# An FFN whose gate and up products run on blocks without the 1/rms factor: one direct chunk instead of two, weight sums by accumulating DMA

## The chip, the cores and the metric

The kernel runs on one core of a Trainium2 chip. The metric is the device time of one execution in microseconds (us); smaller is better. The engines are named as the profile names them: PE (TensorE, matrix products), PEld (its weight loads), DVE (VectorE), ACT (ScalarE), POOL (GpSimd, here used almost only to issue DMAs, among them those that add to what lies in SBUF), and SP (SyncE, which issues plain DMAs).

## The reference

One layer of a streaming encoder over 512 positions of 1024 channels: three token mixers, gated and merged, an output projection with residual, then a SwiGLU FFN with residual. The change is in the FFN and at its seam with the output projection:

```python
D_MODEL = 1024; SEQ = 512; D_FF = 2816
...
x = x + jnp.einsum('bsd,de->bse', merged, w_out[l])

h2 = rms_norm(x, norm_ffn[l])
act = jax.nn.silu(jnp.einsum('bsd,df->bsf', h2, w_ffn_gate[l])) * jnp.einsum('bsd,df->bsf', h2, w_ffn_up[l])
x = x + jnp.einsum('bsf,fd->bsd', act, w_ffn_down[l])
```

with `rms_norm(x, g) = x * rsqrt(mean(x*x) + EPS) * g`, all in float32. The factor 1/rms depends on the position alone, so it may stand before a product or behind it.

## The kernel before

Everything is held transposed: channels on the 128 partitions, the 512 positions along the free dimension. To reach float32 accuracy each operand is split into a high part (ScalarE copies it to `fp32r`) and a low part (VectorE subtracts the high part from the operand), and each product of two tiles is three matmuls: high by high, high by low, low by high. So every weight tile costs a ScalarE and a VectorE step over 128x1024 elements (`split_w` at line 111 and 112, `split_a` at 1403 and 1404), and PE runs three matmuls for each pair of 128x128 weights and 128 channels.

The weights go through a pool of three buffers (`wp`: `raw`, `whi`, `wlo`): a split can begin when the product three earlier has ended. `STEPS` and `OFF` shift the split weights inside their buffers: in each stage of 256-column matmuls the first four weight tiles lie 0, 4, 8 and 12 elements in, all later ones 16.

The output projection (loop over `c` in 0..3, 256 channels each) adds the residual (`x1`, line 1291), and forms x1 times `norm_ffn` without 1/rms as `h2` (high part on ScalarE, line 1294, low part on VectorE, 1295), along with the sum of squares. `rms2` turns this sum into `rb2`, the 1/rms of each position on all partitions, in the background of the first direct chunk.

The FFN's gate and up are made in 11 chunks of 256 hidden channels (of gate and of up each). Two kinds of chunk exist:

- **Direct**, the first `NDIRECT` = 2. `chan_chunk` runs gate (`ps_fg`) and up (`ps_fu`) on `h2`, 512 positions to a matmul: 96 matmuls of 512 columns. The outputs are scaled by `rb2`: gate once before the SiLU, up at the end.
- **Seven products** (`seven`), the other 9. The 256 hidden channels, the 1024 channels and the 512 positions are each halved, and the eight block products are replaced by seven (Winograd's variant of Strassen's scheme), named in `ORDER`: 11, 12, S2, S1, S3, S4, 22. The weight side of each is a block or a sum of blocks of w (S1..S4), for gate and up together; the other side is a block or difference of blocks of the normalised x1 (11, 21, 22, T1..T4: the map is `WITH`). A product is 24 matmuls of 256 columns into the PSUM tiles `ps_y` or `ps_x`; ScalarE copies banks out between products (`tx`, `ty`), and `finish_act` adds the last bank, applies SiLU to the gate and multiplies.

The blocks of the normalised x1 are prepared while PE runs the two direct chunks: background steps (`bg`, popped by `tick`) multiply by `rb2` (`norm2`, line 1336, 16 steps of 128x256), form T1..T4 (`diff_b`, 1347) and split all seven (`split_b`, 1341 and 1342). The weight blocks are loaded by SP, four blocks a chunk in two DMAs each (`load_a`, line 1378, into the eight buffers of `corner`), and their sums S1..S4 are four VectorE steps a chunk (`sums_a`, line 1385). `make_a` splits three products ahead in program order. The engines otherwise follow the order in which a scheduler puts the program's instructions, each engine in order, with weight splits and copies out of PSUM given priority.

Behind the FFN's chunks stands the down projection (`ps_d`, `ps_dx`, `ps_dy`), which already takes its weight sums from accumulating DMAs on POOL (`dadd`, line 1515).

Of the kernel before, what the change touches and what calls it, by code (L numbers as in the profile page):

```python
# [8 lines left out]
F32 = mybir.dt.float32  # L9
F32R = mybir.dt.float32r  # L10
# [16 lines left out]
EARLY = 300  # L27
WARM = 9
GBUFS = 27
NDIRECT = 2  # L30
KD = 10
NTICK = (1, 1)
H = S // 2
# [32 lines left out]

@with_exitstack
def layer_kernel(ctx: ExitStack, tc: tile.TileContext, x, xt, vecs, w_in, w_qkv7, w_gate7, w_pool, w_rg, w_ig,
                 w_branch, w_br7, w_out, w_fg, w_fu, w_fd, w_fd7, out):
    nc = tc.nc  # L70
    act = nc.scalar.activation
    dve = nc.vector
# [39 lines left out]
            dve.tensor_tensor(lo, raw, hi.bitcast(F32), ALU.subtract)  # L112
        return hi, lo

    def add_direct(key, src, a, b):
        def make(n):
            raw = wp.tile([P, a, b], F32, tag="raw", name="raw" + n)
            nc.sync.dma_start(raw, src)
            return split_w(raw, [P, a, b], n)
        specs.append((key, make))  # L120

    def add_chunk256(key, ap, c0):
        add_direct(key + (0,), cols(ap, 0, 4, c0, 256), 4, 256)
        add_direct(key + (1,), cols(ap, 4, 4, c0, 256), 4, 256)

    def add_gate(br, c):
        add_chunk256(("gate", br, c), w_in, 5120 + br * 1024 + c * 256)
# [1128 lines left out]
    with ExitStack() as ffn:  # L1256
# [14 lines left out]

        x1p = {}
        x1 = []
        h2 = []
        for c in range(4):
            xr = g4([2, S], f"xr{c}")
            nc.sync.dma_start(xr, xt[2 * c * P:(2 * c + 2) * P, :].rearrange("(j p) t -> p j t", p=P))
            if c == 0:
                psh = [chunk_psum(("out", n), fp) for n in range(2)]
                for half in range(2):  # L1280
                    for n in range(2):
                        half_chunk(psh[n], ("out", n), half, mt, 0, n == half == 0)
            pss = psh[c] if c < 2 else chan_chunk(("out", c), mt, pool=fp)
            hh = g4([2, S], f"h2h{c}", F32R)
            hl = g4([2, S], f"h2l{c}", F32R)
            for j in range(2):
                k = 2 * c + j
                if c % 2 == 0:
                    x1p[c // 2, j] = mp.tile([P, 2, S], F32, tag="m", name=f"x1{c}{j}")
                t = x1p[c // 2, j][:, c % 2, :]  # L1290
                dve.tensor_tensor(t, pss[j], xr[:, j, :], ALU.add)
                x1.append(t)
                gcol = vcol("norm_ffn", k)
                act(hh[:, j, :], t, AF.Copy, scale=gcol)
                dve.scalar_tensor_tensor(hl[:, j, :], t, gcol, hh[:, j, :].bitcast(F32), ALU.mult,
                                         ALU.subtract)
                h2.append((hh[:, j, :], hl[:, j, :]))
                if k == 0:
                    act(sqsum, t, AF.Square)
                else:  # L1300
                    sq = small(f"sq2{k}", 2, "sq2")
                    act(sq, t, AF.Square)
# [21 lines left out]

        BN = {}
        B = {}

        def norm2(k):  # L1330
            for j in range(2):
                b = BN.setdefault((k // 4, j), None)
                if b is None:
                    b = BN[k // 4, j] = corner([4, H], f"hn{k // 4}{j}")
                js = slice(j * H, (j + 1) * H)
                dve.scalar_tensor_tensor(b[:, k % 4, :], x1[k][:, js], vcol("norm_ffn", k),
                                         rb2[:, js], ALU.mult, ALU.mult)

        def split_b(nm, key, which=0):
            h, l = g4([4, H], f"B{which}{nm}h", F32R), g4([4, H], f"B{which}{nm}l", F32R)  # L1340
            act(h, BN[key], AF.Copy)
            dve.tensor_tensor(l, BN[key], h.bitcast(F32), ALU.subtract)
            B[which, nm] = h, l

        def diff_b(nm, x, y):
            BN[nm] = corner([4, H], f"hn{nm}")
            dve.tensor_tensor(BN[nm], BN[x], BN[y], ALU.subtract)

        def prepare_b():
            nrm = [lambda k=k: norm2(k) for k in range(8)]  # L1350
            return nrm[:4] + [lambda: split_b("11", (0, 0))] + nrm[4:] + [
                lambda: split_b("21", (1, 0)),
                lambda: diff_b("T1", (0, 1), (0, 0)),
                lambda: diff_b("T2", (1, 1), "T1"),
                lambda: split_b("T2", "T2"),
                lambda: split_b("T1", "T1"),
                lambda: diff_b("T3", (1, 1), (0, 1)),
                lambda: split_b("T3", "T3"),
                lambda: split_b("22", (1, 1)),
                lambda: diff_b("T4", (1, 0), "T2"),  # L1360
                lambda: split_b("T4", "T4")]

        SUMS = {"S2": (("S3", "11", "21", ALU.subtract), ("S2", "22", "S3", ALU.subtract)),
                "S1": (("S1", "21", "22", ALU.add),),
                "S4": (("S4", "12", "S2", ALU.subtract),)}

        DOWN = NF // 2
        steps = [(c, nm) for c in range(NDIRECT, DOWN) for nm in ORDER]
        raw = {}
        A = {}  # L1370
        made = [0, NDIRECT]
        offs = []

        def load_a(c):
            for nm in ("11", "21", "22", "12"):
                raw[c, nm] = t = corner([2, 4, P], f"w{c}_{nm}")
                for w in range(2):
                    nc.sync.dma_start(t[:, w], cols((w_fg, w_fu)[w], KH[nm] * 4, 4, c * 256 + CH[nm] * P, P))

        def sums_a(c, nm):  # L1380
            for s_, x, y, op in SUMS.get(nm, ()):
                if (c, s_) in raw:
                    continue
                raw[c, s_] = t = wp.tile([P, 2, 4, P], F32, tag="raw", name=f"w{c}_{s_}")
                dve.tensor_tensor(t, raw[c, x], raw[c, y], op)
# [12 lines left out]

        def split_a(src, n):
            o = offs.pop(0) if offs else OFF  # L1400
# [36 lines left out]
        def seven(c):  # L1437
# [13 lines left out]
            for n, (nm, ps, half, first, t, ts_, src, ss) in enumerate(plan):  # L1451
                make_a(n0 + n + 3)
                product(A.pop((c, nm)), B[0, WITH[nm]], ps, half, first, True)
                if t is not None:
                    act(t[:, :, ts_], src[:, :, ss], AF.Copy)
                if c == DOWN - 1 and nm in PRE:
                    split_d2("11", PRE.index(nm), 0, 0)
                if nm == "S4":
                    finish_act(tx, X, a[:, 0, :])
                if nm == "22":  # L1460
                    finish_act(ty, Y, a[:, 1, :])
            acts.append(a)

        bg.extend([lambda: None, rms2] + prepare_b())
        for c in range(NDIRECT):
            pg = chan_chunk(("fg", c), h2, 3, fp)
            pu = chan_chunk(("fu", c), h2, 3, fp)
            if c == NDIRECT - 1:
                make_a(3)
            a = g4([2, S], f"act{c}")  # L1470
            for j in range(2):
                sg = small(f"sg{c}{j}", 2, "sq2")
                dve.tensor_tensor(sg, pg[j], rb2, ALU.mult)
# [171 lines left out]


_INS = ["x", "xt", "vecs", "w_in", "w_qkv7", "w_gate7", "w_pool", "w_rg", "w_ig", "w_branch", "w_br7", "w_out",
        "w_ffn_gate", "w_ffn_up", "w_ffn_down", "w_down7"]


# [41 lines left out]
```

## Time and profile before

| | before |
|---|---|
| three runs | 898.22, 898.73, 899.13 us; median 898.73 |
| profiled execution, first to last instruction (span) | 896.5 us |
| median less span | 2.2 us |
| PE busy | 891.2 us, 99% |
| PE weight load busy | 795.2 us, 89% |
| VectorE busy | 739.4 us, 82% |
| ScalarE busy | 528.5 us, 59% |
| POOL busy | 88.8 us, 10% |
| granted TensorE clock | 1.00 |

The profiled execution has no device time of its own beside its span: the three runs were made apart from it. The chain that ended last is followed back from the last instruction of the program; where it runs on PE without a gap, PE sets the time there. A PE row's duration in the timeline is the latency of a pipelined matmul: the spacing is the difference between two starts.

### The profile page before, as it was taken

What the parts mean: (1) busy time and instruction counts of PE and PEld (TensorE: products, weight loads), DVE (VectorE), ACT (ScalarE), POOL (GpSimd) and SP (SyncE); (2) the same over time, 40 slices, a digit from 0 to 9 for tenths busy, and PEclk for the clock granted to TensorE, in tenths of its full rate; (3) what the DMA queues carried; (4) which work ended last, traced back from release to release, by engine and by line L of the source; (5) the groups of instructions that cost most, each with busy time, mean ns of one, the idle gap of its engine ahead of it and who ended that gap; (6) DMA issues with size and microseconds to landing.
All of it is one profiled execution on the core that took longest, in us unless ns stands there. A gap on an engine that the chain in (4) does not pass through costs nothing.

```text
span 896.5 us, 14227 instructions
## 1 busy us (share of the span) xinstructions
PE 891.2 (99%) x5563; PEld 795.2 (89%) x5563; DVE 739.4 (82%) x934; ACT 528.5 (59%) x730; POOL 88.8 (10%) x130
## 2 busy tenths in 40 slices
PE   9999999999999999999999999999999999999998
PEld 6888778788889888888888988889999999999998
DVE  6897897997786599967887695699988888899974
ACT  6554989546856556554664544545555555746642
POOL 1110002222323101000001100000000000021200
PEclk9999999999999999999999999999999999999999
DMA  9495336798692785734636865336443343897913
GB/s 337 141 297 167 118 114 215 217 302 252 174 276 72 217 252 175 236 108 152 205 90 154 179 190 170 106 107 169 126 131 104 95 118 97 228 243 195 186 42 118
DMA packets 116644, 154.08 MB, mean 172 GB/s; under 512 B 8161, under 2 KB 90081, under 8 KB 116577
## 3 DMA queue, kind: packets, MB, share of 16 engines
q1 hardware_dynamic: 103904, 107.30, 37.8%
q0 software_dynamic: 12528, 45.62, 21.6%
q8 instruction: 43, 0.70, 0.3%
q10 hardware_dynamic: 144, 0.26, 0.1%
q14 instruction: 25, 0.20, 0.1%
HBM read 132.71 MB, written 18.87 MB: 169 GB/s over the span
## 4 chain that ended last, share of the span: by engine, by line
PE 95%; DVE 2%; ACT 2%; issue 1%; DMA 0%; SPq 0%; DVEq 0%; ACTq 0%
PE ps_y L287 11%; PE ps_x L287 8%; PE ps_q L798 7%; PE ps_dy L1611 6%; PE ps_dx L1611 5%; PE ps_br L278 3%; PE ps_br L279 3%; PE ps_br L280 3%; PE ps_bY L1238 2%; PE ps_gate L701 2%; PE ps_gy L287 2%; PE ps_gate L280 2%; PE ps_bX L1238 2%; PE ps_gx L287 2%; PE ps_gate L278 2%; PE ps_gate L279 2%
## 5 line engine op out<-in xcount | busy, mean ns | idle before, releaser
L111 ACT ACTIVATE whi<-raw 128x1024 fp32r<-128x1024 f32 x69 | 73.1, 1060 | 85.2 <-PE ps_out L279 17.9
L112 DVE TENSOR_TENSOR wlo<-raw,whi 128x1024 fp32r<-128x1024 f32 x69 | 84.4, 1223 | 30.7 <-ACT whi L111 30.7
L112 DVE TENSOR_TENSOR wlo<-qw,whi 128x1024 fp32r<-128x1024 f32 x48 | 58.6, 1224 | 22.0 <-ACT whi L111 21.8
L111 ACT ACTIVATE whi<-qw 128x1024 fp32r<-128x1024 f32 x48 | 50.7, 1059 | 33.2 <-PE ps_q L798 15.3
L1403 ACT ACTIVATE wh_S<-w_S 128x1024 fp32r<-128x1024 f32 x36 | 38.3, 1067 | 34.4 <-PE ps_y L287 22.3
L1404 DVE TENSOR_TENSOR wl_S<-w_S,wh_S 128x1024 fp32r<-128x1024 f32 x36 | 43.8, 1222 | 5.2 <-ACT wh_S L1403 5.1
L1515 POOL DMA_DIRECT2D dw<-in_w_down_dram x20 | 16.9, 847 | 313.6 <-DMA dw<-in_w_down_dram 253.2
L1403 ACT ACTIVATE wh<-w 128x1024 fp32r<-128x1024 f32 x27 | 28.8, 1067 | 30.2 <-issue 11.9
L1404 DVE TENSOR_TENSOR wl<-w,wh 128x1024 fp32r<-128x1024 f32 x27 | 33.0, 1222 | 9.9 <-ACT wh L1403 9.9
L1403 ACT ACTIVATE whdS<-dw 128x1024 fp32r<-128x1024 f32 x20 | 21.3, 1067 | 22.5 <-PE ps_dy L1611 11.0
L1404 DVE TENSOR_TENSOR wldS<-dw,whdS 128x1024 fp32r<-128x1024 f32 x20 | 24.3, 1226 | 6.5 <-ACT whdS L1403 6.4
L1054 DVE TENSOR_TENSOR_SCAN E<-K,ahead 128x512 f32<-128x512 f32 (+3 forms) x32 | 25.4, 815 | 4.4 <-ACT K L1050 4.4
L278 PE MATMUL ps_br<-yHH,whi 128*128 128x512 f32 x64 | 25.3, 395 | 0.0
L278 PE MATMUL ps_lru<-HH,whi 128*128 128x512 f32 x64 | 25.2, 394 | 0.0
L278 PE MATMUL ps_br<-yph,whi 128*128 128x512 f32 x64 | 25.2, 394 | 0.0
L278 PE MATMUL ps_pool<-HH,whi 128*128 128x512 f32 x64 | 25.2, 393 | 0.0
L280 PE MATMUL ps_gate<-HH,wlo 128*128 128x512 f32 x64 | 25.0, 391 | 0.0
L278 PE MATMUL ps_gate<-HH,whi 128*128 128x512 f32 x64 | 25.0, 391 | 0.0
L279 PE MATMUL ps_br<-ypl,whi 128*128 128x512 f32 x64 | 25.0, 391 | 0.0
L280 PE MATMUL ps_br<-yph,wlo 128*128 128x512 f32 x64 | 25.0, 391 | 0.0
L279 PE MATMUL ps_br<-yHL,whi 128*128 128x512 f32 x64 | 25.0, 390 | 0.0
L279 PE MATMUL ps_pool<-HL,whi 128*128 128x512 f32 x64 | 25.0, 390 | 0.0
(737 smaller groups left out, 3448.5 us busy)
## 6 DMA issues: line engine op xcount, KB each, us to landing
raw<-in_w_in_dram SPq DMA_DIRECT2D x31, 512.0 KB, 5.3
qw<-in_w_qkv_dram SPq DMA_DIRECT2D x24, 512.0 KB, 7.4
dw<-in_w_down_dram POOLq DMA_DIRECT2D x20, 512.0 KB, 7.5
w<-in_w_ffn_gate_dram SPq DMA_DIRECT2D x36, 256.0 KB, 4.0
w<-in_w_ffn_up_dram SPq DMA_DIRECT2D x36, 256.0 KB, 4.6
raw<-in_w_branch_dram SPq DMA_DIRECT2D x16, 512.0 KB, 4.1
qw<-in_w_qkv_dram POOLq DMA_DIRECT2D x12, 512.0 KB, 7.7
qd<-r POOLq DMA_DIRECT2D x12, 512.0 KB, 7.9
```

The lines of the kernel that those rows point to most:

```text
L111: act(hi, raw, AF.Copy)
L112: dve.tensor_tensor(lo, raw, hi.bitcast(F32), ALU.subtract)
L278: nc.tensor.matmul(ps, lh, rh, start=start, stop=False, skip_group_check=skip)
L279: nc.tensor.matmul(ps, lh, rl, start=False, stop=False, skip_group_check=skip)
L280: nc.tensor.matmul(ps, ll, rh, start=False, stop=stop, skip_group_check=skip)
L287: nc.tensor.matmul(o, a_[a][:, w, k, :], b_[b][:, k, :], start=first and n == k == 0, stop=last and n == 2 and k == 3, skip_group_check=True)
L798: nc.tensor.matmul(ps[:, a, :], b_[:, k, ts_], a_[:, kk, :], start=first and n == k == 0, stop=n == 2 and k == 3, skip_group_check=True)
L1054: dve.tensor_tensor_scan(E[:, c0:c0 + n][:, ::-1], K[:, c0 + 1:c0 + n + 1][:, ::-1], ahead[:, S - n:][:, ::-1], 0.0, ALU.mult, ALU.add)
L1238: nc.tensor.matmul(o, ah[x_][:, w, k, :], b[k][y_], start=first_ and n == k == 0, stop=n == 2 and k == 3, skip_group_check=True)
L1403: act(h, src, AF.Copy)
L1404: dve.tensor_tensor(l, src, h.bitcast(F32), ALU.subtract)
L1611: nc.tensor.matmul(o, a_[a][:, w, k0 + k, :], b_[b][:, k, :], start=first and i == k == 0, stop=last and i == 2 and k == nk - 1, skip_grou ...
```

## The change

The FFN no longer normalises its blocks. The output projection writes x1 times `norm_ffn`, without 1/rms, in blocks of 128x4x256 (`HR`, by half of the channels and half of the positions), and splits each into high and low part at once (`HB`): these are three of the seven blocks (11, 21, 22), and T1 is formed and split after output chunk 1. T2, T3 and T4 are formed and split in the background of the direct chunk. `finish_act` multiplies the finished gate and up sums by `rb2` (with a sign, since some differences are now formed the other way round). `NDIRECT` is 1: the one direct chunk runs on the same blocks (`block_chunk`, 192 matmuls of 256 columns, position blocks alternating every three matmuls), its four weight tiles carry the offsets of `STEPS`, and the seven-product chunks, now 10, start with offset `OFF`. Their weights come from a new tensor `w_ff7`, laid out on the host block by block; per chunk SP loads 21 into `FX`, 11 into `FY`, and 12 and 22 into raw buffers; POOL's accumulating DMAs make `FX` 21+22, later `FY` 11+21, and `FZ`, which VectorE first sets to `FX`+`FY`, gets 12 added after it was split as S2, to serve as S4.

```diff
-NDIRECT = 2
+NDIRECT = 1
...
+    foffs = list(STEPS)
     for c in range(NDIRECT):
-        add_chunk256(("fg", c), w_fg, c * 256)
-        add_chunk256(("fu", c), w_fu, c * 256)
+        add_chunk256(("fg", c), w_fg, c * 256, foffs)
+        add_chunk256(("fu", c), w_fu, c * 256, foffs)
...
+        def split_b(nm, raw):
+            h, l = g4([4, H], f"B{nm}h", F32R), g4([4, H], f"B{nm}l", F32R)
+            act(h, raw, AF.Copy)
+            dve.tensor_tensor(l, raw, h.bitcast(F32), ALU.subtract)
+            B[0, nm] = h, l
+
+        def diff_b(nm, x, y, sign=1.0):
+            HR[nm] = g4([4, H], f"hr{nm}")
+            if sign > 0:
+                dve.tensor_tensor(HR[nm], HR[x], HR[y], ALU.subtract)
+            else:
+                dve.scalar_tensor_tensor(HR[nm], HR[x], -1.0, HR[y], ALU.mult, ALU.subtract)
...
-                act(hh[:, j, :], t, AF.Copy, scale=gcol)
-                dve.scalar_tensor_tensor(hl[:, j, :], t, gcol, hh[:, j, :].bitcast(F32), ALU.mult,
-                                         ALU.subtract)
-                h2.append((hh[:, j, :], hl[:, j, :]))
+                for tj in range(2):
+                    act(HR[kh, tj][:, k % 4, :], t[:, tj * H:(tj + 1) * H], AF.Copy, scale=gcol)
+            for tj in range(2):
+                h, l = HB[kh, tj]
+                act(h[:, ks, :], HR[kh, tj][:, ks, :], AF.Copy)
+                dve.tensor_tensor(l[:, ks, :], HR[kh, tj][:, ks, :], h[:, ks, :].bitcast(F32), ALU.subtract)
...
+            if c == 1:
+                diff_b("T1", (0, 0), (0, 1))
+                split_b("T1", HR["T1"])
+        B[0, "11"], B[0, "21"], B[0, "22"] = HB[0, 0], HB[1, 0], HB[1, 1]
...
         def prepare_b():
-            nrm = [lambda k=k: norm2(k) for k in range(8)]
-            return nrm[:4] + [lambda: split_b("11", (0, 0))] + nrm[4:] + [
...
+            return [lambda: diff_b("T2", "T1", (1, 1), -1.0),
+                    lambda: split_b("T2", HR["T2"]),
+                    lambda: diff_b("T3", (1, 1), (0, 1)),
+                    lambda: diff_b("T4", "T2", (1, 0), -1.0),
+                    lambda: split_b("T3", HR["T3"]),
+                    lambda: split_b("T4", HR["T4"])]
...
         def load_a(c):
-            for nm in ("11", "21", "22", "12"):
-                raw[c, nm] = t = corner([2, 4, P], f"w{c}_{nm}")
-                for w in range(2):
-                    nc.sync.dma_start(t[:, w], cols((w_fg, w_fu)[w], KH[nm] * 4, 4, c * 256 + CH[nm] * P, P))
-
-        def sums_a(c, nm):
-            for s_, x, y, op in SUMS.get(nm, ()):
-                if (c, s_) in raw:
-                    continue
-                raw[c, s_] = t = wp.tile([P, 2, 4, P], F32, tag="raw", name=f"w{c}_{s_}")
-                dve.tensor_tensor(t, raw[c, x], raw[c, y], op)
+            for nm, buf in (("21", FX), ("11", FY)):
+                buf[c] = t = corner([2, 4, P], f"w{c}_{nm}")
+                nc.sync.dma_start(t, fsrc(c, nm))
+            nc.gpsimd.dma_start(FX[c], fsrc(c, "22"), accum_op=ALU.add)
...
-                if (c, nm) == (NDIRECT, "11"):
-                    offs.extend(STEPS)
                 while made[1] < min(c + 2, DOWN):
                     load_a(made[1])
                     made[1] += 1
-                sums_a(c, nm)
-                A[c, nm] = split_a(raw[c, nm], f"{c}_{nm}")
+                fetch_a(made[0])
+                if nm == "11":
+                    FZ[c] = corner([2, 4, P], f"w{c}_Z")
+                    dve.tensor_tensor(FZ[c], FX[c], FY[c], ALU.add)
+                src = FR.pop((c, nm)) if nm in ("12", "22") else {"1": FY, "S1": FX, "S3": FY}.get(
+                    nm[:1] if nm == "11" else nm, FZ)[c]
+                A[c, nm] = split_a(src, f"{c}_{nm}")
+                if nm == "11":
+                    nc.gpsimd.dma_start(FY[c], fsrc(c, "21"), accum_op=ALU.add)
+                if nm == "S2":
+                    nc.gpsimd.dma_start(FZ[c], fsrc(c, "12"), accum_op=ALU.add)
+                fetch_a(made[0] + 3)
...
-        def finish_act(t, ps, a):
+        def finish_act(t, ps, a, sign):
             dve.tensor_tensor(t, t, ps, ALU.add)
+            dve.scalar_tensor_tensor(t, t, sign, rb2.unsqueeze(1).to_broadcast([P, 2, S]), ALU.mult, ALU.mult)
             act(t[:, 0, :], t[:, 0, :], AF.Silu)
...
+        def block_chunk(key):
+            pss = chunk_psum(key, fp)
+            for half in range(2):
+                wh, wl = weights(*key, half)
+                for j in range(2):
+                    cs = slice(j * P, (j + 1) * P)
+                    for kk in range(4):
+                        for tj in range(2):
+                            h, l = HB[half, tj]
+                            o = pss[j][:, tj * H:(tj + 1) * H]
+                            for n, (w, b) in enumerate(((wh, h), (wh, l), (wl, h))):
+                                nc.tensor.matmul(o, w[:, kk, cs], b[:, kk, :],
...
+                    tick(2)
+            return pss
...
         for c in range(NDIRECT):
-            pg = chan_chunk(("fg", c), h2, 3, fp)
-            pu = chan_chunk(("fu", c), h2, 3, fp)
+            pg = block_chunk(("fg", c))
+            make_a(1)
+            pu = block_chunk(("fu", c))
```

`fetch_a` issues SP's loads of 12 and 22 up to three products ahead; `fsrc` names the block in `w_ff7`.

More of the change, by code (lines that the diff above doesn't have):

```diff
@@ L1283, in layer_kernel @@
             pss = psh[c] if c < 2 else chan_chunk(("out", c), mt, pool=fp)
-            hh = g4([2, S], f"h2h{c}", F32R)
-            hl = g4([2, S], f"h2l{c}", F32R)
+            kh, ks = c // 2, slice(2 * (c % 2), 2 * (c % 2) + 2)
+            if c % 2 == 0:
+                for tj in range(2):
+                    HR[kh, tj] = g4([4, H], f"hr{kh}{tj}")
+                    HB[kh, tj] = [g4([4, H], f"hb{p_}{kh}{tj}", F32R) for p_ in "hl"]
             for j in range(2):
@@ L1387, in make_a, with fetch_a @@
+        def fetch_a(upto):
+            while made[2] < min(upto, len(steps)):
+                c, nm = steps[made[2]]
+                made[2] += 1
+                if nm in ("12", "22"):
+                    FR[c, nm] = t = wp.tile([P, 2, 4, P], F32, tag="raw", name=f"w{c}_{nm}")
+                    nc.sync.dma_start(t, fsrc(c, nm))
         def make_a(upto):
@@ L1658 @@
     nc = _bacc.Bacc("TRN2", target_bir_lowering=False, num_devices=1)
-    lay = {n: inputs[n][0] for n in _INS if n not in ("xt", "vecs", "w_qkv7", "w_gate7", "w_br7", "w_down7")}
+    lay = {n: inputs[n][0] for n in _INS if n not in ("xt", "vecs", "w_qkv7", "w_gate7", "w_br7", "w_ff7", "w_down7")}
     fd = lay["w_ffn_down"]
```

69 lines of the change are left out of this document (24 added, 45 removed).

## The prediction

> **What bounds the kernel now.** I read the page first (parts 1, 2 and 4), then who PE waited for, then PE's timeline at the seams of the FFN, and then VectorE, ScalarE and the DMA issues in the same stretches.
>
> ```profile
> span 896.5 us, 14227 instructions
> PE 891.2 (99%) x5563; PEld 795.2 (89%) x5563; DVE 739.4 (82%) x934; ACT 528.5 (59%) x730; POOL 88.8 (10%) x130
> PEclk9999999999999999999999999999999999999999
> PE 95%; DVE 2%; ACT 2%; issue 1%; DMA 0%; SPq 0%; DVEq 0%; ACTq 0%
> ...
> PE warm_ps L422 <- DVE warm L301: 1.5, 1, 1.5
> PE ps_q L798 <- DVE wlo L112: 0.4, 1, 0.4
> PE ps_gate L701 <- ACT hu L437: 0.3, 1, 0.3
> ```
>
> PE is busy for 891.2 of 896.5 us at the full granted clock, the chain that ended last is PE for 95%, and all its waits in the whole program come to 2.2 us in three places, none in the FFN. So the time is the number of matmuls times their spacing, and an edit can do two things: change that product, or make PE wait where it does not wait now. "Busy" is no spacing, because matmuls overlap; the spacing is read from their starts:
>
> ```profile
> 570.39 0.39 PE L280 MATMUL ps_out<-mth,wlo 128*128 128x512 f32 x1
> 570.62 0.39 PE L278 MATMUL ps_fg<-h2h,whi 128*128 128x512 f32 x1
> ...
> 592.98 0.39 PE L278 MATMUL ps_fg<-h2h,whi 128*128 128x512 f32 x1
> ...
> 614.74 0.28 PE L287 MATMUL ps_y<-B011h,wh 128*128 128x256 f32 x1
> ```
>
> The second direct chunk runs from 592.98 to 614.74: 96 matmuls of 512 columns in 21.76 us, 0.2267 us each. The chain of waits gives the seven-product chunks, 24 matmuls of 256 columns a row:
>
> ```profile
> 614.90 2.87 PE ps_y L287 x24
> 617.77 2.84 PE ps_x L287 x24
> 620.62 2.84 PE ps_y L287 x24
> 623.46 2.83 PE ps_x L287 x24
> 626.28 2.72 PE ps_y L287 x24
> ...
> 639.88 2.72 PE ps_y L287 x24
> ...
> 648.04 2.72 PE ps_x L287 x24
> ```
>
> A settled product takes 2.72 us, 0.1133 us a matmul: half of a 512-column one. The first four products, whose weights lie 0, 4, 8 and 12 elements into their buffers (`STEPS`), take 2.87, 2.84, 2.84 and 2.83, 11.38 us together, 0.50 more than four settled ones.
>
> **PE's own sum.** Two direct chunks go: 2 x 21.76 = 43.52 us. One seven-product chunk comes: 7 x 2.72 = 19.04. One direct chunk comes back as 192 matmuls of 256 columns (two blocks of positions instead of one row of 512). It now carries the four offsets, 48 matmuls on each, and the seven-product chunks start at the settled offset, so their 0.50 goes. Nothing in the trace has 256-column matmuls that change the position block every third one. Bounds: 192 x 0.1133 = 21.76 if it runs settled, and twice the four rows, 2 x 11.38 = 22.76, if the price goes with the offset. I take 22.76: inside the first product the spacing is even from start to end, so it looks like a price per matmul, not a passing one. The sum: 22.76 + 19.04 - 0.50 - 43.52 = **-2.22 us**; with the other bound -3.22.
>
> [...]
>
> **Where PE could begin to wait.** First, the blocks without 1/rms are formed beside the last output-projection chunk.
>
> ```profile
> 570.64 1.06 ACT L111 ACTIVATE whi<-raw 128x1024 fp32r<-128x1024 f32 x1 [4.43 <-PE ps_out L279]
> 571.61 0.71 ACT L1294 ACTIVATE h2h<-x,vt 128x512 fp32r<-128x512 f32 x1
> ...
> 570.82 1.29 DVE L1291 TENSOR_TENSOR x<-ps_out,xr 128x512 f32<-128x512 f32 x2 [3.35 <-PE ps_out L280]
> ...
> 574.42 0.75 DVE L1295 SCALAR_TENSOR_TENSOR h2l<-x,vt,h2h 128x512 fp32r<-128x512 f32 x1
> ...
> L1094 ACT ACTIVATE B11h<-ysb 128x256 fp32r<-128x256 f32 x4 | 1.5, 453 | 0.0
> ```
>
> Before, the low part was ready at 574.42 + 0.75 = 575.17. After, ScalarE does four 256-wide scalings (0.45 each, from the last row) from 571.6, to 573.4, then two 512-wide copies (0.7 each at most) to 574.8, and VectorE's second low part (0.75) ends about 575.6. The second half of the first direct chunk, which needs it, starts after 48 matmuls: 570.62 + 48 x 2.87 / 24 = 576.4. Margin 0.8 us, so nothing is paid; if the squares or a weight split get in between, 0.7 to 1.5 us.
>
> Second, VectorE now has one direct chunk as cover for what it did under two.
>
> ```profile
> 524.20:570.60 46.40, 46.40 (x217) 38.51 (x216) 30.56 (x34) 19.04 (x24) 0.00 (x0) 1.00 0.52 170
> 570.60:592.40 21.80, 21.80 (x97) 17.77 (x96) 19.09 (x32) 10.55 (x13) 0.00 (x0) 1.00 0.24 73
> 592.40:614.70 22.30, 22.30 (x100) 18.48 (x99) 22.30 (x25) 12.77 (x14) 0.00 (x0) 1.00 0.71 190
> 652.90:786.60 133.70, 133.70 (x1182) 133.70 (x1181) 116.97 (x110) 78.05 (x97) 2.92 (x4) 1.00 0.45 128
> ...
> L1336 DVE SCALAR_TENSOR_TENSOR hn<-x,vt,rb 128x256 f32<-128x256 f32 x16 | 6.5, 480 | 0.0
> L1385 DVE TENSOR_TENSOR w_S<-w,w 128x1024 f32<-128x1024 f32 x17 | 20.8, 1225 | 0.5
> 605.46 1.29 DVE L1473 TENSOR_TENSOR sg<-ps_fg,rb 128x512 f32<-128x512 f32 x2
> L666 DVE SCALAR_TENSOR_TENSOR lt<-lr,lt 128x1024 f32<-128x1024 f32 x4 | 4.9, 1223 | 5.5 <-ACT ls L661 5.5
> ```
>
> (A row with a colon gives a stretch, its length, and the busy time of PE, weight load, VectorE, ScalarE and POOL.) T1 and its parts, formed after chunk 1 of the output projection, fall into 46.40 us in which VectorE works 30.56. Over both direct chunks VectorE worked 19.09 + 22.30 = 41.39 us. Gone or moved are 16 normalisations (6.5), five steps on blocks that are now made earlier or not at all (T1's difference and low part, the low parts of 11, 21 and 22: 5 x 1.22), four low parts of the second chunk's weights (4 x 1.22), two weight sums (2.45) and the activation, which falls behind the chunk (3 x 1.29). One sum of weights comes (1.22). 41.39 - 6.5 - 6.1 - 4.9 - 2.45 - 3.9 + 1.2 = 18.7 us in a chunk of 22.8. T2 is wanted by the third product, T4 only by the seventh, 6 x 2.72 us after. So it is hidden, with 4 us to spare.
>
> Third, a settled chunk. 133.70 us are 7.0 chunks, so VectorE works 16.7 of 19.04 us in each. Four weight sums go (4.9), one comes (1.22), and two multiplications by 1/rms on 128x1024 come, at the 1.22 of the row of line 666: 15.5 us. VectorE gets looser. The longer chain behind each product holds no PSUM: the bank is read by the add ahead of the multiplication.
>
> Fourth, the sums by DMA. Per chunk 4 x 2 loads of 256 KB become 4 loads of 512 KB on SP's queue and 3 accumulating ones on POOL's, which did 2.92 us of work in the 133.70.
>
> ```profile
> q1 hardware_dynamic: 103904, 107.30, 37.8%
> q0 software_dynamic: 12528, 45.62, 21.6%
> ...
> 497.00:520.00 23.00, 23.00 (x205) 23.00 (x204) 17.08 (x15) 12.70 (x15) 4.23 (x5) 1.00 0.87 192
> ...
> 635.76 1.22 DVE L1404 TENSOR_TENSOR wl_S<-w_S,wh_S 128x1024 fp32r<-128x1024 f32 x1
> dw<-in_w_down_dram POOLq DMA_DIRECT2D x20, 512.0 KB, 7.5
> bw<-in_w_br_dram POOLq DMA_DIRECT2D x8, 512.0 KB, 5.8
> bw<-in_w_br_dram POOLq DMA_DIRECT2D x1, 512.0 KB, 8.8
> dw<-in_w_down_dram POOLq DMA_DIRECT2D x1, 512.0 KB, 6.1
> dw<-in_w_down_dram POOLq DMA_DIRECT2D x1, 512.0 KB, 9.7
> ```
>
> From the first two rows 512 KB (0.524 MB) hold all engines 1.66 us on SP's queue and 2.22 us on POOL's; 4 x 1.66 + 3 x 2.22 = 13.3 us in 19.04, a share of 0.70. The branch products run at 0.87 with PE busy for all of 23.00 us. The tight one is FZ: 12 is added after S2 is split and S4, three products on, is split from the result. S2's low part ends at 635.76 + 1.22 = 636.98. S4's product starts at 648.04 and its split takes 1.07 + 1.22, so it must start by 645.7. The accumulation has **8.7 us**; here they took 7.5 in the median, 5.8 in the branch stage. POOL's next entry, the accumulation into the coming chunk's FX, waits for a load issued a chunk ahead, and FY's behind it has two products more. I take no wait.
>
> **The rivals.**
>
> *The cover is too short (0.17).* At the seam one of the first two margins fails: the low part comes 1 us late, and the first products wait 1 us more. For it: the margin of 0.8 us goes by rows of other shapes. Against: VectorE's 4 us. -2.22 + 1 to 2 is about 897.9.
>
> *The accumulation lands late (0.12), slower.* It decides at 8.7 us, and each us past that is paid in all ten chunks: ScalarE stands before S4's split, and the copies out of PSUM and 22's split are queued behind it. For it: rows of 8.8 and 9.7 us. Against: the 9.7 us one came while several were issued at once into loaded engines; with spaced ones 6.1. At 9.7 us: 10 x 1.0 - 2.2, about 906.5. [...]
>
> *The fast spacing is not reached (0.04), slower.* If the block chunk's order keeps the products at 2.87 us, 70 x 0.15 = +10.5 us: about 907.
>
> *The offsets cost the block chunk nothing (0.07).* Then the change does more than I say: -3.22, 895.5.
>
> **How the numbers follow.** The forecast has 0.60. The three runs have the median 898.73, 2.2 us above the profiled span of 896.5, and that remainder lies outside the program: 898.73 - 2.22 = **896.5 us**. Its own range is 895.8 to 897.0. A measurement of this kernel tells about 0.2%, 1.8 us, from no change, so the forecast passes it by only 0.4 us. Faster: 0.57 of the forecast and 0.07 of the last rival, 0.64. Within: 0.03 of the forecast and 0.14 of the short cover, 0.17. Slower: 0.03 + 0.12 + 0.04 = 0.19. The range reaches from 895.4 to 900.0 and leaves out most of the two slow cases.
>
> **What would show it.** Right: PE without waits between 524 us and the end, the block chunk's four halves 5.74, 5.68, 5.68 and 5.66 us long, every later product 2.72 us, the first `ps_y` row starting about 593.4, and POOL's accumulations landing under 8.7 us. Wrong: PE waiting on the low part of a block at the second half of the first direct chunk, on T2's at the third product, or ScalarE waiting for a DMA ahead of S4's split in each chunk; or products that stay at 2.8 us.

## The result, and the profile after

The changed kernel took 930.75 us in the median (928.64 to 936.38, four runs) against 898.70 of before on the same chip: a ratio of 1.0366, 95% interval 1.0332 to 1.0401. The forecast was 896.5 with a range that ended at 900.0. The profiled execution (936.38 us, span 934.5) is the slowest of the four. Its page, parts 1, 2 and 4, and who PE waited for:

```profile
span 934.5 us, 14571 instructions
PE 902.9 (97%) x5731; PEld 811.4 (87%) x5731; DVE 724.7 (78%) x910; ACT 533.2 (57%) x750; POOL 115.2 (12%) x160
PEclk9999999999999999999999999899998999999999
PE 82%; DMA 6%; DVE 5%; issue 4%; ACT 3%; ACTq 0%; POOLq 0%; DVEq 0%; SPq 0%
...
PE ps_y L288 <- ACT tx L1464: 17.0, 8, 4.6
PE ps_fg L1484 <- ACT hbh L1318: 5.0, 1, 5.0
PE ps_x L288 <- ACT ty L1464: 1.8, 1, 1.8
...
PE ps_dx L1638 <- DVE wld L1412: 1.1, 2, 0.8
PE ps_fg L1484 <- DVE hbl L1319: 0.8, 1, 0.8
PE ps_y L288 <- DVE wl_S L1412: 0.7, 1, 0.7
```

VectorE is busy for less than before and PE for 12 us more, but PE is no longer the whole chain: 82% of it, and a DMA has 6%. In the FFN, where before had no wait, PE waits 26.4 us in six rows: first in the direct chunk (`ps_fg`, after 60 of its 192 matmuls), then in eight of the ten chunks of seven for ScalarE's copy of a finished bank (`tx`). The granted clock has two dents in the slices; by windows there are four stretches (PEclk is the third number from the end):

```profile
582.40:589.20 6.80, 5.84 (x25) 5.55 (x26) 6.80 (x9) 5.52 (x8) 0.86 (x1) 0.50 0.68 219
637.00:640.40 3.40, 3.37 (x15) 3.37 (x16) 3.12 (x3) 1.41 (x2) 0.00 (x0) 0.51 0.89 140
701.90:708.70 6.80, 5.77 (x27) 5.77 (x28) 3.59 (x3) 2.87 (x5) 0.85 (x1) 0.50 0.63 145
790.60:794.00 3.40, 3.40 (x18) 3.40 (x18) 1.19 (x1) 0.42 (x1) 0.00 (x0) 0.51 0.56 197
```

So PE ran 20.4 us at half its clock, each stretch beginning within about 1 us of the end of a wait: up to 10 us more of loss. The chain of waits shows both places. First the seam of the output projection and the direct chunk, then the first chunk that is hit and the next one:

```profile
568.31 8.94 DMA w<-in_w_ff_dram
...
583.94 5.28 PE ps_fg L1484 x23
...
591.18 11.34 PE ps_fu L1484 x96
602.51 2.73 PE ps_y L288 x24
...
627.21 8.12 DMA w_Z<-in_w_ff_dram
...
636.40 0.59 ACT tx L1464
...
637.03 4.61 PE ps_y L288 x24
...
658.95 0.59 ACT tx L1464
...
659.58 3.01 PE ps_y L288 x24
```

The first product starts at 602.51 where 593.4 was forecast: about 9 us lost at the seam, which the waits of 5.0 and 0.8 and half of 6.8 us at half clock make up. The ten chunks take 219.6 us (to 822.1) instead of 70 x 2.72 = 190.4, 29.2 more: 19.5 of waits (17.0, 1.8, 0.7), 6.8 for the 13.6 us at half clock, and 2.9 left over. Most of that is the first product behind a wait, which the chain gives as 3.01 instead of 2.72 us (659.58 us above); four products at 2.83 us add 0.4.

**Who stands ahead of whom.** VectorE at the seam and in the first chunk that is hit, and ScalarE there, by their timelines:

```profile
577.32 1.23 DVE L1397 TENSOR_TENSOR w_Z<-w,w 128x1024 f32<-128x1024 f32 x1 [8.17 <-DMA w<-in_w_ff_dram]
...
579.60 1.28 DVE L1311 TENSOR_TENSOR x<-ps_out,xr 128x512 f32<-128x512 f32 x2
...
624.02 1.22 DVE L1439 SCALAR_TENSOR_TENSOR ty<-ty,rb 128x1024 f32<-128x1024 f32 x1
625.16 1.22 DVE L1412 TENSOR_TENSOR wl_S<-w_Z,wh_S 128x1024 fp32r<-128x1024 f32 x1
...
626.97 1.06 ACT L1411 ACTIVATE wh_S<-w 128x1024 fp32r<-128x1024 f32 x1 [0.52 <-ACT tx L1464]
635.44 1.06 ACT L1411 ACTIVATE wh_S<-w_Z 128x1024 fp32r<-128x1024 f32 x1 [7.40 <-DMA w_Z<-in_w_ff_dram]
636.40 0.58 ACT L1464 ACTIVATE tx<-ps_y 128x512 f32<-128x512 f32 x1
```

How long the ten accumulations into `FZ` took from issue to landing, by the view of that tile:

```profile
DMA to landing us min/median/max: 5.1/5.6/8.1
```

At the seam the first `FZ` sum of the chunks of seven stands on VectorE in front of the residual additions of the last output chunk. It needs `FX` with 22 added; that DMA was issued at 568.31 and took 8.94 us, and VectorE stood for 8.17 us with the additions, the scaling, the split and PE behind it. In the chunks S4's split stands on ScalarE in front of the copy `tx` of S2's bank, which S3's product, the next but one, needs: 7.40 us of ScalarE waiting for the accumulation into `FZ`. That was issued at 627.21, once the low part of S2 was done (625.16 + 1.22), and the low part had stood behind the multiplications by 1/rms. (The profile names a ScalarE copy that ended within 0.1 us of it as what the issue waited for; that the low part decides is shown below, where moving it alone moves the issue.)

### The profile page after: what moved, and what is told of

Read it like the earlier page. It is cut to its first block, busy times and chain, and to the rows that moved or that the text cites. A ratio compares the mean times of both kernels' runs of the same rounds, so it can differ in the third digit from the quotient of the medians.

```text
span 934.5 us, 14571 instructions
## 1 busy us (share of the span) xinstructions
PE 902.9 (97%) x5731; PEld 811.4 (87%) x5731; DVE 724.7 (78%) x910; ACT 533.2 (57%) x750; POOL 115.2 (12%) x160
## 4 chain that ended last, share of the span: by engine, by line
PE 82%; DMA 6%; DVE 5%; issue 4%; ACT 3%; ACTq 0%; POOLq 0%; DVEq 0%; SPq 0%
PE ps_y L288 8%; PE ps_q L799 7%; PE ps_x L288 6%; PE ps_dy L1638 5%; PE ps_dx L1638 4%; DMA w_Z<-in_w_ff_dram 4%; PE ps_br L279 3%; PE ps_br L280 3%; PE ps_br L281 3%; PE ps_bY L1239 2%; PE ps_gy L288 2%; PE ps_gate L702 2%; PE ps_gate L281 2%; PE ps_bX L1239 2%; PE ps_gx L288 2%
## 5 line engine op out<-in xcount | busy, mean ns | idle before, releaser
L111 ACT ACTIVATE whi<-raw 128x1024 fp32r<-128x1024 f32 x65 | 68.8, 1058 | 75.4 <-PE ps_br L280 14.7
L112 DVE TENSOR_TENSOR wlo<-raw,whi 128x1024 fp32r<-128x1024 f32 x65 | 79.3, 1220 | 32.3 <-ACT whi L111 32.3
L111 ACT ACTIVATE whi<-qw 128x1024 fp32r<-128x1024 f32 x48 | 50.7, 1057 | 33.1 <-PE ps_q L799 18.7
L1412 DVE TENSOR_TENSOR wl_S<-w_Z,wh_S 128x1024 fp32r<-128x1024 f32 x20 | 24.5, 1223 | 43.5 <-ACT wh_S L1411 43.5
L1411 ACT ACTIVATE wh_S<-w_Z 128x1024 fp32r<-128x1024 f32 x20 | 21.2, 1061 | 60.2 <-DMA w_Z<-in_w_ff_dram 30.3
L1411 ACT ACTIVATE wh<-w 128x1024 fp32r<-128x1024 f32 x30 | 31.8, 1060 | 35.2 <-PE ps_y L288 19.1
L1412 DVE TENSOR_TENSOR wl<-w,wh 128x1024 fp32r<-128x1024 f32 x30 | 36.6, 1222 | 16.8 <-ACT wh L1411 16.6
L288 PE MATMUL ps_y<-BT3h,wh_S 128*128 128x256 f32 x80 | 25.6, 321 | 17.0 <-ACT tx L1464 17.0
L288 PEld LDWEIGHTS ps_y<-BT3h,wh_S 128*128 128x128 f32 x80 | 17.6, 220 | 18.6 <-ACT tx L1464 18.6
L1411 ACT ACTIVATE wh_S<-w 128x1024 fp32r<-128x1024 f32 x20 | 21.3, 1066 | 16.6 <-issue 10.8
L1412 DVE TENSOR_TENSOR wl_S<-w,wh_S 128x1024 fp32r<-128x1024 f32 x20 | 24.1, 1222 | 1.7 <-ACT wh_S L1411 1.7
```

What stands on the lines that cost most here:

```text
L111: act(hi, raw, AF.Copy)
L288: nc.tensor.matmul(o, a_[a][:, w, k, :], b_[b][:, k, :], start=first and n == k == 0, stop=last and n == 2 and k == 3, skip_group_check=True)
L1411: act(h, src, AF.Copy)
L1412: dve.tensor_tensor(l, src, h.bitcast(F32), ALU.subtract)
```

## The experiments

**The two places, one at a time.** The theory: both losses are places in a queue where one instruction waits for an accumulating DMA and path work stands behind it. The rival: the change costs this in any order, by the DMAs' traffic or by VectorE's load.

First, the second accumulation replaced by a sum on VectorE:

```diff
-nc.gpsimd.dma_start(FZ[c], fsrc(c, "12"), accum_op=ALU.add)
+dve.tensor_tensor(FZ[c], FZ[c], FR[c, "12"], ALU.add)
```

> The changed kernel, but S4's sum (FZ plus block 12) is a VectorE step instead of an accumulating DMA; FX and FY still come from DMA. Theory A (PE waits in every seven-product chunk because FZ's accumulation lands late and ScalarE stands before S4's split with the copy of the PSUM bank queued behind it): the waits of PE on tx in the chunks go, VectorE does about 16.7 us in a chunk of 19.04, and the ten chunks fall from 219.7 us to about 190: 902 us, the seam's loss staying. Theory B (the waits come from the general DMA load, or from the longer chain behind each product with its two multiplications by 1/rms): two of three accumulations and both multiplications are still there, so 920 us or more.

909.55 us (908.83 to 911.90), ratio 1.0132 [1.0117, 1.0147]. All waits on `tx` and `ty` are gone, though VectorE has ten steps more, and the chunks take 191.4 us; the seam's waits (5.2, 0.8) stay. The cause that the first theory names is confirmed, its number missed: it took the chunks' 29 us, read in the slowest run of 936.38, off the median of 930.75, and in this run the down stage fell to a slow pace (below).

Second, the seam alone: the first sum is kept behind what stands before it in the program.

```diff
-dve.tensor_tensor(FZ[c], FX[c], FY[c], ALU.add)
+z = dve.tensor_tensor(FZ[c], FX[c], FY[c], ALU.add)
+if c == NDIRECT:
+    tc.keep_in_program_order(z)
```

> The changed kernel, but the first chunk's sum FX+FY is held in program order on VectorE, behind the preparation of the blocks, so that it cannot stand ahead of the last residual adds. Theory A (the seam loses about 9 us because VectorE waits for the DMA into FX with the residual adds, and so the blocks, queued behind that wait): PE's 5.8 us of waits in the first direct chunk go and the half clock after them too, about 922 us. Theory B (the blocks themselves come late, through ScalarE's four scalings and two copies): PE still waits on the blocks' parts in the first direct chunk, 928 us or more.

922.98 us (920.69 to 924.98), ratio 1.0276 [1.0258, 1.0294]: 7.8 us back, the waits of `ps_fg` gone, those on `tx` left (14.7 us): by the first theory.

Third, the accumulation kept, but S4's split on ScalarE kept behind the copies (in `split_a`, to which the name `nm` is handed as well):

```diff
-act(h, src, AF.Copy)
+i = act(h, src, AF.Copy)
+if nm == "S4":
+    tc.keep_in_program_order(i)
```

> The changed kernel, but ScalarE's split of S4 is held behind the copy of the bank after S2 (tx); the accumulation into FZ is as late as before. Theory A, part 1 (what PE waits for is the copy queued behind the waiting split): S4's deadline moves from the S3 product to its own, 2.72 us later; accumulations that land in 5.5 us no longer cost anything, those of 8 us cost about 2: 905 to 915 us, and the remaining waits of PE are on wh_S or wl_S and stand before the S4 product. Rival (the landing itself is too late for S4's own product): the waits only move by one product, 925 us or more.

916.65 us (914.63 to 920.76), ratio 1.0199 [1.0182, 1.0216], 14.1 us back. The waits on `tx` are gone, 3.0 us on `ty` are left, and from 657 us to the last chunk every product took 2.83 us: the theory's band was missed by 2 us, for a reason that neither side had.

The first and second edits together:

> Both edits: S4's sum on VectorE and the first FX+FY sum held in program order. Theory A: PE has no waits in the FFN, the direct chunk takes 22.8 us and the ten chunks 190.4 us: 896 to 898 us, a little under the kernel before. Theory B (something else, such as the down projection's accumulations behind the FFN's on POOL, costs too): above 900 us, with the rest in PE's waits after the FFN.

900.70 us (899.98 to 902.47), ratio 1.0033 [1.0020, 1.0046]. So 30 of the 34 us over the forecast are these two places; alone the edits gave 21.2 and 7.8. The first theory's 896 to 898 was missed: PE still waits 0.7 us in the last chunk and 0.9 us in the down stage. Its chain of waits, from the first product into the down stage:

```profile
594.84 2.73 PE ps_y L288 x24
...
771.63 1.15 DVE wl_S L1414
...
772.82 2.79 PE ps_y L288 x22
...
811.79 6.58 DMA dr<-in_w_down_dram
```

**Is the accumulating DMA itself too slow?** The accumulation kept, with the second and third edits, without and with a higher priority for S2's low part on VectorE (so that it goes ahead of part of the chunk's finish and the accumulation is issued sooner):

```diff
 i = act(h, src, AF.Copy)
...
-dve.tensor_tensor(l, src, h.bitcast(F32), ALU.subtract)
+with tc.high_priority(60 if nm == "S2" else 0):
+    dve.tensor_tensor(l, src, h.bitcast(F32), ALU.subtract)
```

> Keeps the accumulating DMA; the seam is mended and S4's split stands behind the copies out of PSUM, but S2's split is where the change has it. Theory A (the two orders are worth what they were worth alone, 7.8 and 14.1 us, and the slow pace of 2.83 us a product that followed the second alone comes from a wait that is still there): 908 to 909 us. Rival B (the pace in the second alone came from the waits at the seam): every product at 2.72 us, and about 901 us as in the version that also advanced S2's split.

> Keeps the accumulating DMA into the settled sum. Three orders are changed: the first sum of two weight quarters is kept behind the work of the seam on VectorE, S4's split is kept behind the copies out of PSUM on ScalarE, and S2's split is put ahead of the finish of the chunk before. Theory A (the lost time is order in the queues, not the transfer): the seam gives back 7.8 us as in the run with the seam alone, the copies no longer wait, and the accumulation is issued some 3 us earlier, so S4's split meets it: 898 to 904 us, no wait of a product on tx or ty over 1 us. Rival B (the landing of the accumulation, 5.5 to 8.9 us, is too long in any order): waits of S4's product on its own weight parts in most chunks, and 907 us or more.

Without the priority 907.60 us (906.64 to 909.19), ratio 1.0101 [1.0087, 1.0115], 0.4 us under the band of the first theory, and the two orders are worth together what they were worth alone (23.2 against 21.9): one wait of 2.2 us on `ty` in the last chunk, and the pace of 2.83 us from 630 us on. No wait of PE stands ahead of that change of pace, so the theory's reason for it is not shown. With it 900.65 us (899.53 to 908.69), ratio 1.0043 [1.0025, 1.0061], as good as the sum on VectorE, with no wait of PE in the chunks over 0.2 us. In the third chunk the accumulation is issued at 637.12 us, 2.2 us ahead of S2's product, and without the priority at 638.43 us, 0.2 us ahead of it. All three accumulations and both multiplications by 1/rms are still there, so the rival of traffic or of VectorE's load is out. The transfer is not too slow for the kernel; it was too slow for its place. But the ten runs spread over 9 us, and the profiled one was the slowest of them:

```profile
605.58 2.72 PE ps_y L288 x24
608.30 2.94 PE ps_x L288 x24
611.25 5.65 PE ps_y L288 x48
```

One spacing of 0.22 instead of 0.11 us, and this product's other matmuls and the following products to 761 us take the slow pace, 2.83 us a product, without a wait and at clock 1.00.

**The pace.** The chunks' products settle at one of two spacings, 113.3 or 117.8 ns a matmul. What sets which? The version with the seam mended and the sum on VectorE (900.70), with the block chunk's weights at offset 16 from the start:

```diff
-foffs = list(STEPS)
+foffs = []
```

> The version without the second accumulation and with the seam mended (900.7 us), but the block chunk's weights lie at the offset of 16 from the first one on. Theory A (the offset sets the spacing of the matmuls): the block chunk takes 21.76 us, 96 matmuls in 10.9 and not 11.34 us, and the run 899.7 us; the products behind it stay at 2.72 us. Rival B (the spacing is a state that the four steps of offset bring about): the block chunk stays at 22.7 us, and the products behind it run at 2.83 us or more, which over ten chunks of seven is 7.7 us: about 908 us.

909.34 us (907.40 to 910.96), ratio 1.0121 [1.0108, 1.0134]: the second theory, though the block chunk itself took 11.52 us a half, more than with the four offsets (11.34). And the same with the four offsets given to the first four products of the chunks of seven (`offs = list(STEPS)`):

> As the run with the block chunk's weights at the offset of 16 throughout (909.3 us, all products at 2.83 us), but the first four products of the chunks of seven take their weights at the offsets 0, 4, 8 and 12. Theory A (a walk through the four offsets, wherever it stands, sets the pace of what follows): the fifth and later products take 2.72 us, 66 products by 0.11 us or 7.3 us less, about 902 us. Rival B (the pace was set before, at the block chunk's start): 2.83 us to the end of the chunks, about 909 us.

902.46 us (901.27 to 904.84), ratio 1.0050 [1.0032, 1.0069]: the first theory. Two chains, first of the offset 16 throughout, then of the walk:

```profile
583.42 11.52 PE ps_fu L1486 x96
594.94 2.83 PE ps_y L288 x24
...
756.06 2.83 PE ps_x L288 x24
```

```profile
594.59 2.88 PE ps_y L288 x24
...
603.15 2.83 PE ps_x L288 x24
605.98 2.72 PE ps_y L288 x24
...
758.30 2.72 PE ps_y L288 x24
```

With the walk through 0, 4, 8, 12 the products behind run at 2.72 us, without it at 2.83 us for the whole stage, though the weights of all lie at offset 16. So the pace is not the price of an offset: it is a state that lasts, and in these two runs the walk decides it. The walk is not the only thing that changes it. In the changed kernel the slow pace followed the half clock at 708 us and ended at a wait of 0.9 us, with no walk there:

```profile
719.92 2.83 PE ps_y L288 x24
...
725.86 0.59 ACT tx L1464
...
729.50 2.72 PE ps_x L288 x24
```

The same happened behind a wait of 1.3 us (798 us) in the version with S4's split kept behind the copies. Two direct chunks, both on blocks, show that a walk does not fix what comes behind it either:

> The version without the second accumulation and with the seam mended (900.7 us), but with two direct chunks again, both on blocks. By the prediction's sum the second block chunk, at the buffer offset of 16, costs 192 x 113.3 ns = 21.76 us and a chunk of seven products 7 x 2.72 = 19.04 us, so 2.7 us more: 903.4 us. If the block form costs 22.76 us at any offset: 904.4 us. Rival (what is left is VectorE's load, which a direct chunk eases): under 901.5 us.

910.82 us (909.85 to 911.85), ratio 1.0138 [1.0123, 1.0153], over both bands. The first block chunk takes the walk (11.34 us for `fu`), the second, at 16, runs at 11.52 a half from its start, and all products behind it at 2.83: 2 x 11.52 - 19.04 + 63 x 0.11 = 10.9 us over the 900.70; the run shows 10.1. Products of the chunks of seven that stand right behind the walk were fast, a block chunk in that place was not; why was not separated.

**The last 4 us.** The 900.70 us version has two late steps left: VectorE forms the direct chunk's low part `al` among the finish of a chunk (0.7 us of wait), and the down stage waits for a load whose raw buffer came free at 811.7 us. Four versions, each with the seam mended and the sum on VectorE. With `al` one chunk earlier and the priority of S2:

> The version without the second accumulation (sum by VectorE) and with the seam mended, 900.7 us, and besides that the low part of the direct chunk's activations is formed one chunk earlier and S2's split goes ahead of the finish. Theory A (what is left over 898.7 us is VectorE's queue around the start of the down stage): the wait of 0.7 us before the last S product goes, the first waits in the down stage shrink by up to the 1.2 us moved: 899.0 to 900.0 us. Rival B (what is left are transfers that come late because the raw buffers are held): 900.7 us and the same waits of ps_dx on the weights' low parts.

900.79 us (900.46 to 904.43), ratio 1.0038 [1.0024, 1.0053]. The wait on `wl_S` is gone, but S2's split now stood in front of a copy (1.4 us on `tx`), and the waits of `ps_dx` are as they were (1.0 against 0.9 us): the rival's number. With `al` one chunk earlier, no priority, and two of the `dr` loads in the activations' pool:

```diff
-wp.tile([P, 2, 4, P], F32, tag="raw", name=f"dr{nm}{n}")
+(g4([2, 4, P], f"dr{nm}{n}") if nm == "12" and n > 2 else
+ wp.tile([P, 2, 4, P], F32, tag="raw", name=f"dr{nm}{n}"))
```

> The version without the second accumulation and with the seam mended (900.7 us), and two things more: the low part of the direct chunk's activations is formed one chunk earlier, and the fourth and fifth weight loads of the down stage's second product go into buffers of the activations' pool, not into the three raw buffers, so that they needn't wait for the first of them to be split. Theory A (what is left of the loss is that step on VectorE, about 1 us, and the raw buffer that comes free at 811.7 us, whose load lands 6.6 us later, about 2 us): the wait before the last S product and the waits of ps_dx on wld go, 897.5 to 898.5 us. Rival B (the down stage stays late through VectorE's own queue): 899.5 us or more, with the waits on wld as they were.

899.58 us (898.28 to 904.35), ratio 1.0019 [1.0007, 1.0030]. It is in the rival's band, for another reason. The wait for the load is gone, but in the profiled run (902.15, well above the median) the down stage ran at the slow pace, 28.27 us for 240 matmuls instead of 27.20, and `al` made the same 0.7 us wait one chunk earlier. So a second walk there (`if dmade[0] in (1, 11)`), and `al` on GpSimd:

> The version with the two loads of the down stage in the activations' pool (899.6 us), with the low part of the direct chunk's activations formed by GpSimd and not by VectorE, and with a second walk of the weight offsets through 0, 4, 8 and 12 at the fifteen-matmul pieces of the down stage's third product. Theory A (what is left is the wait of 0.7 us and a down stage that fell to the slow pace after its waits, 28.3, 28.3, 14.1 and 10.6 us where 27.2, 27.2, 13.6 and 10.2 are the fast ones, 3 us in all): 896.5 to 898.0 us, with a spread of the runs under 2 us. Rival B (the pace cannot be set again there, or GpSimd holds up the accumulating DMAs behind it): 899 us or more.

900.09 us (899.32 to 901.43), ratio 1.0020 [1.0011, 1.0029]. The row was 27.20 again, and the 11 runs spread over 2 us where the 12 before had spread over 6. That fits a walk that sets the pace, but versions without the second walk also reached 27.20 there (the one of 900.70 did), so one trace does not show it. GpSimd cost more than it saved; its timeline row, and VectorE's that stood beside it:

```profile
749.51 3.34 POOL L1512 TENSOR_TENSOR al<-act,ah 128x1024 fp32r<-128x1024 f32 x1 [4.65 <-ACT ah L1511]
...
750.51 3.42 DVE L1414 TENSOR_TENSOR wl_S<-w_Z,wh_S 128x1024 fp32r<-128x1024 f32 x1
```

VectorE's step of 1.22 us took 3.42: it ended 1.1 us after GpSimd's (753.93 against 752.85), and PE waited 1.4 us on `wl_S`. Last, `al` back on VectorE, pinned in the middle of the last chunk but one:

> As the version with the second walk of the offsets (900.1 us), but the low part of the direct chunk's activations is formed by VectorE, not GpSimd, and pinned behind the weight splits in the middle of the last chunk but one, not beside the finish of the chunk before. Theory A (the 1.4 us wait and the slower product after it, 1.6 us in all, came from GpSimd and VectorE standing in each other's way at 749.5 to 752.9 us, and the step has room in the middle of a chunk): no wait on wl_S, 898.0 to 898.8 us. Rival B (VectorE has no room anywhere in these chunks): the same wait at another product, 899.3 us or more.

898.13 us (897.47 to 898.85), ratio 0.9996 [0.9987, 1.0006]: as the first theory said, and no difference from before that can be told. Its chain, of the slowest of the 11 runs:

```profile
583.94 11.34 PE ps_fu L1488 x96
595.27 2.73 PE ps_y L288 x24
...
785.68 0.23 PE ps_d L279
...
811.24 13.89 PE ps_dx L1642 x120
825.15 14.12 PE ps_dx L1642 x118
839.27 27.20 PE ps_dy L1642 x240
```

## Why the prediction was wrong

**PE's own sum held in size, not in its reason.** `fu` takes 11.34 us, half of 22.76 to within 0.04, and the products behind run at 2.72. In the last version the stretch from the start of the direct chunk to the down stage is 785.68 - 571.52 = 214.16 us, before it was 786.76 - 570.62 = 216.14: -1.98, where the sum said -2.22. But the price does not go with the offset, as the prediction had it: at offset 16 throughout the block chunk was no faster (11.52 us a half), and the products behind it, at their settled offset, were slow. That the 0.50 us went, and that the 22.76 came, is a matter of the state of the pace, which the prediction did not know: the size came out right by luck, for a reason other than the one given.

**"First" and "Second" failed at the seam by what they left out.** The margin of 0.8 us and VectorE's cover were counted in VectorE's own work, and with the seam mended PE waits for none of it. Of "Second" that was right with less to spare: VectorE works 21.1 us in that stretch, where 18.7 was forecast. Of "First" it was luck. In the version of 900.70 us the low part ended at 578.18 us, 2.1 us later after the start of the direct chunk than forecast, because VectorE's residual additions came later, behind a weight split; and PE reads the first piece of it after 60 matmuls, not 48, so the margin came out at 0.6 to 0.8 us all the same. Two rows of that version's timeline:

```profile
576.89 1.29 DVE L1319 TENSOR_TENSOR hbl<-hr,hbh 128x512 fp32r<-128x512 f32 x2
...
578.37 0.28 PE L1486 MATMUL ps_fg<-hbl,whi 128*128 128x256 f32 x1
```

What was left out is that the first `FZ` sum may be put ahead of the residual additions while its operand is still on its way. The prediction followed the moved steps, and this one it counted as "One sum of weights comes (1.22)". It cost VectorE not 1.22 but 8.17 us more of standing, and 7.8 us of the whole, as the run with the seam alone shows.

**"Third" held as far as it went.** VectorE is not the bound in a settled chunk: 15.5 us were forecast, 15.2 measured (the version with the priority), and even with one step more a chunk the products run without a wait. Its longer finish mattered in the last chunks, where `al` joins it.

**"Fourth" is the step that failed most.** It took the deadline of the accumulation from S4's product, three products on, and found 8.7 us. Two things in it were wrong. The deadline is the copy of S2's bank, which stands behind S4's split on ScalarE and which S3's product, the next but one after S2's, needs: S3 could have started at 637.03 - 4.6 = 632.4, less 0.6 for the copy and 1.06 for the split, 630.7. And the start is not the end of S2's split as it was before, 2.9 us ahead of S2's product, but 627.21, at about its start, since the low part now stands behind the finish of the chunk before. That leaves 3.5 us, and these landed 5.1 to 8.1 us after their issue (the one of 627.21 after 8.12, 4.6 us too late, which is the wait). The second rival named the very queue ("ScalarE stands before S4's split, and the copies out of PSUM and 22's split are queued behind it") and still kept the 8.7 us, with which it decided against itself.

**The size of a wait was too small.** The rival's price was 1 us of time for 1 us of wait. The waits here came with half clock for 20.4 us (in the version of 900.70 us, without them, the clock was 1.00) and, in one stretch, the slow pace: with 26.4 us of waits the profiled span grew by 38 us. The third rival (the fast spacing not reached, 2.87 us) had a lasting slow spacing, but as a fixed property of the block order; the products behind that order did reach the fast pace, and in several versions lost it later.

**What remains without a wait.** In the last version the gain of 1.98 us is there and is spent again in the profiled run: the direct chunk begins 0.9 us later (571.52 against 570.62), and the down stage takes 1.7 us longer (111.4 against 109.7 from its first matmul to the end of the span). The first is no cost of the change as far as is known: in the profiles of the changed kernel and its versions that start lies anywhere from 570.3 to 571.5. Of the second, 0.8 is the second walk (13.89 + 14.12 against 27.20). Whether the rest is the later loads of the down stage, which share the eight buffers with one more tile a chunk, was not separated.

## What to carry to other kernels

When a sum is handed from an engine to an accumulating DMA, count its deadline not from the product that uses it but from the first instruction that is queued behind the one that waits for it: here path work stood behind a wait of 7.40 us on ScalarE and one of 8.17 us on VectorE. Keeping the two waiting instructions in program order behind path work gave back 23 of the 34 us over the forecast, and issuing the transfer 2 us sooner brought that to 30. Why the scheduler had put them so early was not looked into. And where PE had no waits at all, waits cost more than their length: here 26.4 us of them came with 38 us of span.

## What was not expected of the hardware

The clock fell to half (0.50 or 0.51) for 3.4 or 6.8 us at or just behind waits of PE of 5.0, 4.6, 3.0 and 1.8 us, but not behind five others of 0.9 to 1.9 on `tx`, where it read 1.00. The length of a wait alone did not decide it: behind the one of 1.80 us (until 789.64) the clock was 0.51 for 3.4 us, behind one of 1.88 us (until 768.51) it stayed at 1.00. What else decides was not shown.

In these runs the 256-column matmuls had two lasting spacings at full clock, 113.3 and 117.8 ns (2.72 and 2.83 us for 24), and a block chunk at offset 16 ran at a third, 120.0 ns (11.52 us for 96). Four products with weights at the offsets 0, 4, 8 and 12 brought the first for the products right behind them (902.46 against 909.34 us); one spacing of 0.22 us stands where it was lost (608.30 us above), and a wait of 0.9 us where it came back (725.86). The slow pace over a whole stage is 66 x 0.11 = 7.3 us, which is most of the 9 us by which the runs of one kernel differ (899.53 to 908.69); but only the slowest of them has a trace. What in the machine holds this state is open.

Beside a GpSimd subtraction that reads two tiles one VectorE step took 3.42 us: this step, 1.22 us elsewhere, ended at 753.93, 1.1 us after GpSimd's 752.85. VectorE's step just ahead of it (749.38 us) had overlapped the same GpSimd row for 1.1 us and still took 1.22. Why the one was held up and the other was not is not shown.
